# A gated recurrence in tiles of 128 tokens: a seventh pairing level and four state steps instead of eight

## The chip, the cores and the metric

The kernel runs on one core of a Trainium2 chip: TensorE (PE; its weight loads are shown apart as PEld), VectorE (DVE), ScalarE (ACT), GpSimd (POOL), and SyncE (SP), which issues most DMAs. The metric is the device time of one execution, in microseconds (us).

## The reference, cut to what matters

Two layers of an encoder with three token mixers side by side (A: latent attention, B: a gated linear recurrence, C: differential attention), gates, a projection, and a gated MLP. 512 prompt tokens and 8 requests of 16 sample tokens go through every layer, 640 tokens in all. The change is in branch B alone. Per head (8 heads, 64 key and 64 value channels), with f the forget gate of a token and channel:

```
def step(S, blk):
    qb, kb, vb, gb = blk                          # gb = log f
    b = jnp.cumsum(gb, axis=1)
    o_inter = jnp.einsum('blhk,bhkv->blhv', qb * jnp.exp(b), S)
    dec = ...                                     # exp(b_t - b_s) for s <= t, else 0
    att = jnp.einsum('bthk,btshk,bshk->bhts', qb, dec, kb)
    o_intra = jnp.einsum('bhts,bshv->bthv', att, vb)
    S = jnp.exp(b_last)[..., None] * S + jnp.einsum(
        'bshk,bshv->bhkv', kb * jnp.exp(b_last[:, None] - b), vb)
```

So a state S of 64x64 per head is carried from block to block; inside a block each token sees the earlier ones through weights that hold the decays between them. How long a block is does not change the result.

## The kernel before, in words

**The streams.** Each layer is written as four streams: A, B, C and G (the gates' projections, `stream_g`). The string `ORDER` says which stream is advanced next. What is written is not yet the order of execution: the tile framework plans each engine's queue from the dependencies, its own costs and the free buffers, earlier written work first. Each engine then runs its queue in order. So projections (line 123, groups of 24 matmuls of 320 or 256 columns, fp32 split into a high and a low part) stand between the recurrence's matmuls wherever the planner saw a gap. After the streams come the mix (branch projections under their gates, lines 1112 to 1149), the output projection and the MLP.

**Branch B** (`stream_b`) goes over two units of four heads, and in each over two pairs of heads: eight pairs over two layers. The two heads of a pair lie in the upper and lower 64 partitions of q, k and the decays F, tokens along the free dimension (640). `qz` holds q twice, each time zero in the other head's partitions.

*Levels* (lines 978 to 1002). Within blocks of 64 tokens the weights are built by doubling. At level H (1, 2, 4, 8, 16, 32) the right half of a block of 2H sees its left half: matmuls of k against qz (line 985, 64 columns each) give all weights of a chunk, a predicated copy (line 990) takes those of this level into `at`, then q of the right halves is multiplied by the decay of the left (line 995, one head on VectorE, one on GpSimd), k of the left halves by the decay of the right (line 996), and the decays of two halves are multiplied (line 998). `at` holds the weights as [128, 10, 64]: for each token tile and head the 64x64 block of either chunk.

*Chunks* (lines 1006 to 1034). q of both heads is added into one tile, k is transposed (line 1011) and copied to `kt_`. Eight chunks of 64 follow: what the state gives to the chunk (line 1021), weights times values for each head (line 1023), the state's increase (line 1026), and on VectorE for each head the new state (line 1031: old state times decay plus increase; line 1033 in the first chunk). The matmuls of a chunk use the upper or the lower 64 partitions of a tile. After that come norm, output, and the sample requests' states (lines 1035 to 1080).

Buffers come from rings by tag: `pd` has 13 of [128, 640], `sc` three banks of PSUM, `a` three tiles. `copy` (line 90) goes to ScalarE and VectorE in turn.

Of the kernel before, what the change touches and what calls it, by code (L numbers as in the profile page):

```python
# [19 lines left out]
SEQ = 512  # L20
# [10 lines left out]
class Cols:  # L31
    """tiles [128, n], one a block, read as one [128, k, n]."""
# [21 lines left out]
def body(ctx: ExitStack, tc: tile.TileContext, i, o, depth=DEPTH):  # L54
# [74 lines left out]
    def norm_T(xs, gsrc, xh, xl, stag="st"):  # L129
        """rms of token-major halves xs[h] [128, NT, 512] -> split transposed xh, xl, each [128, 4, TOK] x2; a tile a call."""  # L130
        gb = [T("e", [128, 512]) for _ in range(2)]
        for h in range(2):
            SY.dma_start(gb[h][:], gsrc[h * 512:(h + 1) * 512].partition_broadcast(128))

        def tile_(t):
            st = T(stag, [128, 16])
            cs = slice(t * 128, (t + 1) * 128)
            for h in range(2):
                A.activation(xh[h][:, :, cs], xs[h][:, t].rearrange("p (k n) -> p k n", k=4), AF.Square, accum_out=st[:, h:h + 1])
            V.tensor_tensor(st[:, 2:3], st[:, 0:1], st[:, 1:2], op=ALU.add)  # L140
            rstd(st[:, 3:4], st[:, 2:3], D)
            for h in range(2):
                xn = T("t", [128, 512])
                V.scalar_tensor_tensor(xn[:], xs[h][:, t], st[:, 3:4], gb[h][:], op0=ALU.mult, op1=ALU.mult)  # L144
                ps = P("tp")
                for k in range(4):
                    PE.transpose(ps[:, k * 128:(k + 1) * 128], xn[:, k * 128:(k + 1) * 128], ident[:])  # L147
                pv = ps[:].rearrange("p (k n) -> p k n", k=4)
                hi = xh[h][:, :, cs]
                if isinstance(xl[h], Cols):  # L150
                    A.copy(hi, pv)
                    for k in range(4):
                        V.tensor_tensor(xl[h][:, k, cs], pv[:, k], hi[:, k].bitcast(F32), op=ALU.subtract)  # L153
                else:
                    split(hi, xl[h][:, :, cs], pv)
        return tile_
# [4 lines left out]
    def projB(w, c0, xh, xl, evac, tag="mm", hs=(0, 1)):  # L161
        """feature-major: columns c0..c0+128 of the unit, all tokens in two halves."""
        for h in hs:
            ps = P(tag)
            prs = []
            cs = slice(h * HT, (h + 1) * HT)
            for u in range(len(w)):
                hi, lo = w[u]
                for k in range(4):
                    a, b = hi[:, k, c0:c0 + 128], lo[:, k, c0:c0 + 128]  # L170
                    prs += [(a, xh[u][:, k, cs]), (a, xl[u][:, k, cs]), (b, xh[u][:, k, cs])]
            mm3(ps[:, :HT], prs)
            evac(h, ps[:, :HT])
# [10 lines left out]
    def tok_out(l, t, name, ap_fn):  # L184
        """DMA a token tile: prompt rows or sample rows."""

    def constants():
# [28 lines left out]
        # hgrn lower bound: softmax over depth, running sum less the first  # L216
# [30 lines left out]
    for l in range(depth):  # L247
# [15 lines left out]
        # ---- input norm  # L263
# [21 lines left out]
        def put_T(dst_, cols, tok):  # L285
            """transpose a token-major [128, 512] tile into feature-major columns."""
            ps = P("tp")
            for k in range(4):
                PE.transpose(ps[:, k * 128:(k + 1) * 128], tok[:, k * 128:(k + 1) * 128], ident[:])
            copy(dst_[:, :, cols], ps[:].rearrange("p (k n) -> p k n", k=4))  # L290

        def headnorm(on, ps, n, st, rs=None):
            """rms over groups of 64 of ps [128, n * 64] (PSUM), each over its rs where given, without the gain."""
            sq = T("t", [128, 512])
            A.activation(sq[:, :n * 64], ps, AF.Square)
            V.tensor_reduce(st[:, 0:n], sq[:, :n * 64].rearrange("p (h d) -> p h d", d=64), axis=AX.X, op=ALU.add)
            scaled_rstd(st[:, 0:n], n, rs)
            V.tensor_tensor(on, ps.rearrange("p (h d) -> p h d", d=64), bc(st[:, 0:n], 64), op=ALU.mult)

        def scaled_rstd(v, n, rs):  # L300
            """rstd of v / rs^2 over 64, times 1 / rs (rs in its first n columns, the next n are scratch)."""
            if rs is None:
                rstd(v, v, 64)
                return
            r = rs[:, n:2 * n]
            V.reciprocal(r, rs[:, 0:n])
            for _ in range(2):
                V.tensor_tensor(v, v, r, op=ALU.mult)
            rstd(v, v, 64)
            V.tensor_tensor(v, v, r, op=ALU.mult)  # L310
# [6 lines left out]
        # == gates  # L317
        gpark = {}

        def stream_g():  # L320
            """branch gates, parked in DRAM until their branch is there."""
            for n in (0, 2, 1):
                for u in range(4):
                    wg = wload2(W_in, C_G + n * D + u * 256)
                    for c in range(2):
                        sg = T("g", [128, TOK])

                        def ev(h, ps):
                            A.activation(sg[:, h * HT:(h + 1) * HT], ps, AF.Tanh, scale=0.5)
                        projB(wg, c * 128, xh, xl, ev)  # L330
                        gp = dp.tile([128, TOK], F32, name=f"gp{l}_{n}_{2 * u + c}", tag=f"gp{l}_{n}_{2 * u + c}")[:]
                        SY.dma_start(gp, sg[:])
                        gpark[n, 2 * u + c] = gp
                    yield

        # ---- branch A: latent attention
        def stack_k(dst_, src):
            """32 rows of keys as 96: high, high, low (against queries' high, low, high)."""
# [4 lines left out]
        def stream_a():  # L343
# [48 lines left out]
            def a_latents(t):  # L392
# [13 lines left out]
                # rotary key  # L406
# [7 lines left out]
                # queries  # L414
# [19 lines left out]
            for t in range(NT):  # L434
# [5 lines left out]
                for hf in range(2):  # L440
# [21 lines left out]
                    else:  # L462
# [4 lines left out]
                        for bq in range(2):  # L467
                            # rows: high, low, high
# [26 lines left out]
            # == A keys and values  # L495
# [48 lines left out]
            # == A prompt attention  # L544
# [28 lines left out]
            # == A sample requests, against the latent rows  # L573
# [81 lines left out]
        # ---- branch C: differential attention  # L655
        def stream_c():
# [21 lines left out]
            def c_inproj(u):  # L678
                """queries and keys of two blocks; high and low parts of the prompt's go to DRAM."""
# [44 lines left out]
            def c_stack(blk, hh):  # L724
                """a head's two queries and keys as 96 rows: high, low, high against high, high, low."""
# [11 lines left out]
            # == C prompt attention  # L737
# [4 lines left out]
            def p_probs(un, q):  # L742
                """a head's weights for a block of queries, over the first softmax's scale."""
# [59 lines left out]
            # == C sample requests  # L803
# [69 lines left out]
            for bh in range(2):  # L873
# [8 lines left out]
                # each row holds two heads' values; its own half counts  # L882
# [22 lines left out]
        # ---- branch B: gated recurrence  # L905
        def stream_b():
            ob = kept["ob"] = T("ob", [128, 4, TOK])
            late = None
            for u in range(2):
# [39 lines left out]
                for c in range(2):  # L949
# [5 lines left out]
                    # == B diagonal and levels  # L955
# [18 lines left out]
                    # qz holds each head's q (zero in the other head's rows) with its decay from the start of its block, k that to the end of its block, F a block's whole decay  # L974
# [3 lines left out]
                    for li, H in enumerate(LEVELS):  # L978
# [23 lines left out]
                        fo += nb  # L1002
                    if late:
                        late()
                    yield
                    G.tensor_tensor(q[:], qz[c][:, 0], qz[c][:, 1], op=ALU.add)
                    # == B chunks
# [10 lines left out]
                    for ch in range(SEQ // 64):  # L1018
                        t, cs = ch // 2, slice(ch % 2 * 64, ch % 2 * 64 + 64)
                        if ch:  # L1020
                            PE.matmul(ov[cs, t * 128:(t + 1) * 128], lhsT=q[:, ch * 64:(ch + 1) * 64], rhs=S[:], start=True, stop=False)
                        for hh in range(2):
                            PE.matmul(ov[cs, t * 128 + hh * 64:t * 128 + (hh + 1) * 64], lhsT=at[cs, 2 * t + hh],
                                      rhs=hv_[t][cs, c * 128 + hh * 64:c * 128 + (hh + 1) * 64], start=(ch == 0), stop=(ch == 0 or hh == 1))
                        sp = P("tp")
                        PE.matmul(sp[:, :128], lhsT=kt_[cs, t], rhs=hv_[t][cs, c * 128:(c + 1) * 128], start=True, stop=True)
                        Sn = Sbd[2 * c + ch % 2]
                        for hh in range(2):
                            hs = slice(hh * 64, (hh + 1) * 64)
                            if ch:  # L1030
                                V.scalar_tensor_tensor(Sn[hs, hs], S[hs, hs], Fc[hs, ch:ch + 1], sp[hs, hs], op0=ALU.mult, op1=ALU.add)
# [21 lines left out]
                    # == B sample states  # L1053
# [30 lines left out]
        # the branches and gates are traced interleaved, each string's letter advancing its own  # L1084
# [27 lines left out]
        # == mix: branch projections under their gates  # L1112
# [38 lines left out]
        # ---- output projection and residual  # L1151
# [22 lines left out]
        # ---- gated MLP with causal convolution  # L1174
# [89 lines left out]
        # == down projection  # L1264
# [9 lines left out]
        for s in range(2):  # L1274
# [13 lines left out]
            # the token tiles end one after the other  # L1288
# [18 lines left out]
    # ---- final norm  # L1307
# [75 lines left out]
```

## Time and profile before

| | us |
|---|---|
| median of 3 runs | 2901.35 (2899.43 to 2904.15) |
| span of the profiled execution | 2904.4 |
| its own time around the span | not shown by the page |
| PE busy / PEld busy | 2835.3 / 2542.7 |
| DVE / ACT / POOL busy | 1472.6 / 987.4 / 352.5 |

A matmul in fp32 shows as two instructions (64 matmuls of a line appear as x128). Matmuls are pipelined and their ends are modelled, so that in an order of time the distance from start to start is the cost, not the duration. The page's slices:

```profile
PE   7999999999999999999999999999999999999998
DVE  5465464355565544443454654633646545444444
PEclk9999999999999999999999999999999999999999
```

Each digit is a fortieth of the span (73 us) in tenths. Layer 0's recurrence lies from 622 to 839 us (slices 9 to 12), layer 1's from 2060 to 2270 (slices 29 to 32). The eight pairs, as the sums below take them, are 622 to 668, 668 to 709, 765 to 805, 805 to 839, 2060 to 2100, 2100 to 2142, 2193 to 2233 and 2233 to 2270 us; between the units lie projections alone.

### The profile page before, as it was taken

The numbers are of one execution on the slowest core, as the hardware profiler recorded it, in microseconds if no ns is written. First come the engines' busy times: TensorE is split into PE (matmuls) and PEld (weight loads), VectorE is DVE, ScalarE is ACT, GpSimd is POOL, SyncE is SP. The second block draws the span as 40 slices with busy tenths as digits, with TensorE's granted clock in tenths as the row PEclk, the third lists the DMA queues.
The fourth block names the chain that finished last, engine by engine and source line by source line (L and its number), as shares of the span: only waits on it lengthen the run. The fifth ranks groups of instructions, "written<-read, shape, count | busy, mean of one in ns | idle before, by whom it ended". The sixth has DMA issues, their size and how long they took to land. (4 is left out here: it accounts for less than half of the span.)

```text
span 2904.4 us, 48551 instructions
## 1 busy us (share of the span) xinstructions
PE 2835.3 (98%) x19600; PEld 2542.7 (88%) x19600; DVE 1472.6 (51%) x3117; ACT 987.4 (34%) x2074; POOL 352.5 (12%) x559
## 2 busy tenths in 40 slices
PE   7999999999999999999999999999999999999998
PEld 7979997778889999998899799977788899999976
DVE  5465464355565544443454654633646545444444
ACT  4444453232221322222444443623222223222332
POOL 1000120012122001000000011200222210110000
PEclk9999999999999999999999999999999999999999
DMA  4213563322244222222333136443232442222222
GB/s 147 69 50 110 169 173 115 118 89 82 80 140 155 74 73 73 73 85 76 98 110 93 41 120 184 122 141 116 82 98 66 154 134 70 73 77 81 86 73 73
DMA packets 297996, 293.66 MB, mean 101 GB/s; under 512 B 51493, under 2 KB 254765, under 8 KB 296237
## 3 DMA queue, kind: packets, MB, share of 16 engines
q1 hardware_dynamic: 290092, 277.97, 31.1%
q0 software_dynamic: 7680, 12.59, 1.8%
q8 instruction: 155, 2.54, 0.4%
q14 instruction: 69, 0.56, 0.1%
HBM read 245.37 MB, written 44.09 MB: 100 GB/s over the span
## 5 line engine op out<-in xcount | busy, mean ns | idle before, releaser
L99 DVE TENSOR_TENSOR wl<-wr,wh 128x1024 fp32r<-128x1024 f32 (+2 forms) x292 | 370.6, 1270 | 339.1 <-ACT wh L98 336.3
L98 ACT CAST wh<-wr 128x1024 fp32r<-128x1024 f32 (+2 forms) x292 | 305.1, 1045 | 605.9 <-PE sc L123 213.0
L123 PE MATMUL mm<-xh,wh 128*128 128x320 f32 x1280 | 409.0, 320 | 0.0
L123 PE MATMUL mm<-xl,wh 128*128 128x320 f32 x1280 | 408.1, 319 | 0.0
L123 PE MATMUL mm<-xh,wl 128*128 128x320 f32 x1280 | 405.2, 317 | 0.0
L123 PE MATMUL sc<-ob,wh 128*128 128x320 f32 x1568 | 400.6, 310 | 2.9 <-DVE pd L1142 2.9
L123 PE MATMUL mm<-wh,xh 128*128 128x256 f32 (+1 forms) x960 | 281.2, 293 | 6.6 <-ACT xh L1148 3.9
L123 PE MATMUL mm<-wh,xl 128*128 128x256 f32 (+1 forms) x960 | 280.4, 292 | 1.1 <-DVE xl L99 1.0
L123 PE MATMUL mm<-wl,xh 128*128 128x256 f32 (+1 forms) x960 | 280.8, 293 | 0.0
L123 PEld LDWEIGHTS sc<-ob,wh 128*128 128x128 f32 x1568 | 275.1, 188 | 3.7 <-DVE pd L1142 3.7
L123 PE MATMUL mm<-ob,wh 128*128 128x320 f32 (+1 forms) x1088 | 275.1, 312 | 1.2 <-ACT ob L98 0.6
L123 PE MATMUL sc<-ob,wl 128*128 128x320 f32 x832 | 257.6, 310 | 0.0
L123 PEld LDWEIGHTS mm<-xh,wh 128*128 128x128 f32 x1280 | 243.0, 190 | 7.2 <-issue 3.1
L123 PEld LDWEIGHTS mm<-xh,wl 128*128 128x128 f32 x1280 | 242.6, 190 | 6.3 <-issue 3.4
L123 PEld LDWEIGHTS mm<-xl,wh 128*128 128x128 f32 x1280 | 242.9, 190 | 4.9 <-issue 0.4
L123 PE MATMUL mm<-ob,wl 128*128 128x320 f32 (+1 forms) x720 | 224.7, 312 | 0.0
L123 PE MATMUL sc<-pd,wh 128*128 128x320 f32 x608 | 189.3, 311 | 3.4 <-DVE pd L1142 3.4
L123 PEld LDWEIGHTS mm<-wh,xh 128*128 128x128 f32 x960 | 184.1, 192 | 9.3 <-ACT xh L1148 4.3
L123 PEld LDWEIGHTS mm<-ob,wh 128*128 128x128 f32 x1088 | 189.4, 188 | 2.9 <-DVE ob L99 1.1
L123 PEld LDWEIGHTS mm<-wh,xl 128*128 128x128 f32 x960 | 183.8, 192 | 1.7 <-DVE xl L99 1.2
L123 PEld LDWEIGHTS mm<-wl,xh 128*128 128x128 f32 x960 | 184.1, 192 | 1.1 <-issue 0.8
L123 PEld LDWEIGHTS sc<-ob,wl 128*128 128x128 f32 x832 | 156.2, 188 | 0.0
(379 smaller groups left out, 5218.3 us busy)
## 6 DMA issues: line engine op xcount, KB each, us to landing
wr<-in_w_in_dram SPq DMA_DIRECT2D x104, 512.0 KB, 4.2
wr<-in_ffn_w_up_dram SPq DMA_DIRECT2D x88, 512.0 KB, 3.6
wr<-in_ffn_w_down_dram SPq DMA_DIRECT2D x44, 512.0 KB, 3.6
pd<-in_cache_diff_k_dram SPq DMA_DIRECT2D x64, 256.0 KB, 3.8
pd<-in_cache_diff_v_dram SPq DMA_DIRECT2D x64, 256.0 KB, 3.2
gp<-g SPq DMA_DIRECT2D x48, 320.0 KB, 3.8
pd<-gp SPq DMA_DIRECT2D x48, 320.0 KB, 3.8
wr<-in_w_branch_dram SPq DMA_DIRECT2D x24, 512.0 KB, 3.6
```

The source lines that it names most:

```text
L98: a = A.copy(hi, src)
L99: v = V.tensor_tensor(lo, src, hi.bitcast(F32), op=ALU.subtract)
L123: PE.matmul(out, lhsT=a, rhs=b, start=(j == 0), stop=(j == n - 1))
```

## The change

After the sixth level a seventh joins the two chunks of a tile. Four matmuls (one a tile, both heads' q of the right chunk against k of the left) go into one bank of PSUM. The weights then get a buffer of their own for each head, `ap_[z]` [128, 4, 128], from the ring `pd`: ScalarE copies the two diagonal blocks of 64x64 from `at` (for all tiles at once), GpSimd sets the lower left block to zero, and `copy` takes the upper right one from PSUM. q of the right chunks, k of the left ones and the decays are updated as at any level. The chunk loop then has four steps over tiles of 128 tokens: reading the state, weights times values and the state's increase each use all 128 partitions. What is written for the sample requests, which end at level 8, is the same. The rest of the diff takes comments and docstrings out.

```diff
@@ -1000,11 +1000,32 @@
                             tot = fx[:, fo + SEQ // 16:fo + SEQ // 16 + NB]
                         Fc = Fn
                         fo += nb
+
+                    ps = P("sc")
+                    for t in range(4):
+                        PE.matmul(ps[:64, t * 128:(t + 1) * 128], lhsT=k[:, t * 128:t * 128 + 64], rhs=qz[c][:, :, t * 128 + 64:(t + 1) * 128],
+                                  start=True, stop=True)
+                    ap_ = [T("pd", [128, 4, 128]) for _ in range(2)]
+                    for z in range(2):
+                        az = at[:, 0:8].rearrange("p (t z) n -> p z t n", z=2)[:, z]
+                        for ch in range(2):
+                            r = slice(ch * 64, (ch + 1) * 64)
+                            A.copy(ap_[z][r, :, r], az[r])
+                        G.memset(ap_[z][64:128, :, 0:64], 0.0)
+                        copy(ap_[z][0:64, :, 64:128], ps[:64].rearrange("p (t z n) -> p z t n", t=4, z=2)[:, z])
+                    fv = Fc[:, :8].rearrange("p (n two) -> p n two", two=2)
+                    v4 = lambda tl: tl[:, :SEQ].rearrange("p (n two h) -> p n two h", two=2, h=64)
+                    for z in range(2):
+                        qv = v4(qz[c][:, z])[:, :, 1]
+                        (G if z else V).tensor_tensor(qv, qv, bc(fv[:, :, 0], 64), op=ALU.mult)
+                    V.tensor_tensor(v4(k)[:, :, 0], v4(k)[:, :, 0], bc(fv[:, :, 1], 64), op=ALU.mult)
+                    Fc = fx[:, fo:fo + 4]
+                    V.tensor_tensor(Fc, fv[:, :, 0], fv[:, :, 1], op=ALU.mult)
                     if late:
                         late()
                     yield
                     G.tensor_tensor(q[:], qz[c][:, 0], qz[c][:, 1], op=ALU.add)
-                    # == B chunks
+
                     kt_ = T("e", [128, NT, 128])
                     tp = P("tp")
                     for t in range(4):
...
@@ -1015,20 +1036,19 @@
                     copy(kt_[:, 4], tp[:, :128])
                     ov = P("ov")
                     S = None
-                    for ch in range(SEQ // 64):
-                        t, cs = ch // 2, slice(ch % 2 * 64, ch % 2 * 64 + 64)
-                        if ch:
-                            PE.matmul(ov[cs, t * 128:(t + 1) * 128], lhsT=q[:, ch * 64:(ch + 1) * 64], rhs=S[:], start=True, stop=False)
+                    for t in range(4):
+                        if t:
+                            PE.matmul(ov[:, t * 128:(t + 1) * 128], lhsT=q[:, t * 128:(t + 1) * 128], rhs=S[:], start=True, stop=False)
                         for hh in range(2):
-                            PE.matmul(ov[cs, t * 128 + hh * 64:t * 128 + (hh + 1) * 64], lhsT=at[cs, 2 * t + hh],
-                                      rhs=hv_[t][cs, c * 128 + hh * 64:c * 128 + (hh + 1) * 64], start=(ch == 0), stop=(ch == 0 or hh == 1))
+                            PE.matmul(ov[:, t * 128 + hh * 64:t * 128 + (hh + 1) * 64], lhsT=ap_[hh][:, t],
+                                      rhs=hv_[t][:, c * 128 + hh * 64:c * 128 + (hh + 1) * 64], start=(t == 0), stop=(t == 0 or hh == 1))
                         sp = P("tp")
-                        PE.matmul(sp[:, :128], lhsT=kt_[cs, t], rhs=hv_[t][cs, c * 128:(c + 1) * 128], start=True, stop=True)
-                        Sn = Sbd[2 * c + ch % 2]
+                        PE.matmul(sp[:, :128], lhsT=kt_[:, t], rhs=hv_[t][:, c * 128:(c + 1) * 128], start=True, stop=True)
+                        Sn = Sbd[2 * c + t % 2]
                         for hh in range(2):
                             hs = slice(hh * 64, (hh + 1) * 64)
-                            if ch:
-                                V.scalar_tensor_tensor(Sn[hs, hs], S[hs, hs], Fc[hs, ch:ch + 1], sp[hs, hs], op0=ALU.mult, op1=ALU.add)
+                            if t:
+                                V.scalar_tensor_tensor(Sn[hs, hs], S[hs, hs], Fc[hs, t:t + 1], sp[hs, hs], op0=ALU.mult, op1=ALU.add)
                             else:
                                 V.tensor_copy(Sn[hs, hs], sp[hs, hs])
                         S = Sn
```

## Rows read from the trace of the kernel before

**Rows 1.** the page's busy times: busy us, share of the span, instructions.
```profile
PE 2835.3 (98%) x19600; PEld 2542.7 (88%) x19600; DVE 1472.6 (51%) x3117; ACT 987.4 (34%) x2074; POOL 352.5 (12%) x559
```

**Rows 2.** table by stage, sums over the eight pairs; all engines, then line 123.
```profile
sum 320.00, PE 306.16 PEld 249.97 DVE 213.39 ACT 68.13 POOL 94.75; mean PE 38.27 PEld 31.25 DVE 26.67 ACT 8.52 POOL 11.84
...
sum 320.00, PE 162.12 PEld 133.09; mean PE 20.27 PEld 16.64
```

**Rows 3.** order of time on PE, end of layer 0's recurrence (start, us, instruction).
```profile
838.94 0.27 PE L1049 MATMUL tp<-ident,t 128*128 128x128 f32 x1
838.96 0.54 PE L123 MATMUL sc<-ob,wh 128*128 128x320 f32 x2
```

**Rows 4.** order of time on PE, one chunk step of the first pair.
```profile
650.73 0.43 PE L1021 MATMUL ov<-Sbd,pd 128*64 128x128 f32 x2
651.09 0.44 PE L1023 MATMUL ov<-ob,a 64*64 64x64 f32 x4
651.47 0.48 PE L1026 MATMUL tp<-ob,e 64*128 64x128 f32 x2
651.88 0.41 PE L123 MATMUL mm<-xl,wh 128*128 128x320 f32 x1
```

**Rows 5.** order of time on PE, runs of full-array fp32 matmuls.
```profile
228.77 1.14 PE L634 MATMUL tp<-a,pd 128*128 128x128 f32 x8
229.74 0.39 PE L634 MATMUL tp<-a,ckv 128*128 128x128 f32 x2
229.97 1.06 PE L634 MATMUL tp<-a,pd 128*128 128x128 f32 x8
230.86 0.39 PE L634 MATMUL tp<-a,ckv 128*128 128x128 f32 x2
```

**Rows 6.** costliest groups on PE: out<-in, shapes, count | busy us, mean ns | idle before.
```profile
L568 PE MATMUL ov<-a,pd 128*64 128x128 f32 x320 | 31.4, 285 | 0.0
L1023 PE MATMUL ov<-ob,a 64*64 64x64 f32 x256 | 29.2, 236 | 0.0
L1026 PE MATMUL tp<-ob,e 64*128 64x128 f32 x128 | 26.2, 331 | 0.0
L1021 PE MATMUL ov<-Sbd,pd 128*64 128x128 f32 x112 | 25.0, 307 | 0.1
```

**Rows 7.** costliest groups on DVE, ACT and POOL, same columns.
```profile
L1031 DVE SCALAR_TENSOR_TENSOR Sbd<-Sbd,e,tp 64x64 f32<-64x64 f32 x112 | 31.3, 279 | 45.4 <-PE tp L1026 42.9
L995 DVE TENSOR_TENSOR qz<-qz,e 128x256 f32<-128x256 f32 x16 | 10.2, 640 | 0.0
L996 DVE TENSOR_TENSOR pd<-pd,e 128x256 f32<-128x256 f32 x16 | 6.6, 412 | 0.0
L95 DVE COPY t<-sc 64x256 f32<-64x256 f32 x4 | 1.6, 406 | 0.0
L998 DVE TENSOR_TENSOR e<-e 128x8 f32<-128x8 f32 x8 | 1.3, 160 | 0.1
...
L93 ACT COPY t<-sc 64x256 f32<-64x256 f32 x4 | 1.4, 360 | 0.8 <-PE sc L1059 0.8
...
L995 POOL TENSOR_TENSOR qz<-qz,e 128x256 f32<-128x256 f32 x16 | 10.4, 651 | 25.5 <-PE sc L985 17.3 <-issue 5.0 <-DVE e L998 1.7
L840 POOL MEMSET e<- 128x128 f32 x32 | 6.6, 206 | 303.4 <-PE tp L860 172.6 <-DVE e L850 88.5 <-ACT a L93 12.5
```

**Rows 8.** order of time on PE: a level that waits, and a step at half clock.
```profile
670.68 0.82 PE L985 MATMUL sc<-qz,pd 128*64 128x64 f32 x20 [0.56 <-DVE pd L996]
...
690.48 0.69 PE L1021 MATMUL ov<-Sbd,pd 128*64 128x128 f32 x2
...
692.43 0.69 PE L1021 MATMUL ov<-Sbd,pd 128*64 128x128 f32 x2
```

**Rows 9.** table by stage: slice, length, PE, PEld, DVE, ACT, POOL, clock, DMA share, GB/s.
```profile
690.00:700.00 10.00, 10.00 (x49) 6.88 (x47) 1.96 (x7) 1.64 (x2) 0.00 (x0) 0.50 0.02 3
...
2140.00:2150.00 10.00, 10.00 (x74) 10.00 (x74) 1.58 (x6) 2.26 (x6) 0.70 (x1) 0.83 0.55 199
```

More of the change, by code (lines that the diff above doesn't have):

```diff
@@ L184, in tok_out @@
     def tok_out(l, t, name, ap_fn):
+        pass
     def constants():
```

## The prediction

> **What bounds the kernel now.** Three views, in this order. First the page's busy times [rows 1]: TensorE is busy for 98% of the span, VectorE for half, ScalarE for a third, GpSimd for an eighth. So the first question about any edit is what it does to TensorE's own work. Second, the table by stage over the eight stretches in which a pair of heads goes through the recurrence, four in each layer [rows 2]: 320 us, TensorE busy 306 of them, so it stands for 14 us only; VectorE 213, ScalarE 68, GpSimd 95. The same table for the projection line alone shows why: 162 of the 306 us are matmuls of the projections that the planner laid between the recurrence's own. They go on to the end: 20 ns after the stretch's last transpose the branch projections begin [rows 3]. There is always something to put into a gap, so the time of this stage is the sum of TensorE's work, and a microsecond of it saved is a microsecond of the whole. Third, the order of time on TensorE within a chunk step [rows 4]: reading the state, weights times values and the new state's product follow each other without a gap, 1.15 us for the eight instructions of a step (each fp32 matmul shows as two).
>
> **What the state steps cost and will cost.** Now: eight steps a pair at 1.15 us, less the state product that the first step lacks (0.37): 8.8 us of TensorE. Each of the three groups uses part of the array (128x64, 64x64, 64x128) and every change from one to the next shows: two instructions of 128 columns take 0.36 to 0.41 us.
> After: four tiles of 128 tokens, all on the full array, 6 + 3 x 8 = 30 instructions. The full-array row with as many columns is the latent attention's output [rows 5]: eight instructions from 228.77 to 229.74 (0.121 each), eight from 229.97 to 230.86 (0.111). So 30 instructions cost 3.3 us at the least. At the most each tile costs what a step's groups cost today, with the weights' four at 0.45: 4 x 1.23 - 0.37 = 4.6. I take 3.9 (0.13 each): the rows of full-array runs are nearer, since all three groups now have one shape, but the groups stay short and are entered from 320-column projections.
>
> The Trainium skill, TensorEngine Tiling (Array Packing), section Key Properties, says that a change of tiling mode drains the engine. By that rule alone a tile would cost eight times 0.111, 0.9 us, and the gain would grow by some 4 us over the eight pairs; the trace agrees in kind (0.18 to 0.2 us an instruction where the mode changes, 0.11 where it does not) [rows 4, 5].
>
> **The new level.** Four matmuls a pair, eight instructions, 64 columns of weights against 128 columns. No row shows this shape alone. From below: prompt attention's 128*64 form, two halves side by side, 31.4 us busy for 320, 0.10 each [rows 6], 0.8 us. From above: 0.18 each as in the state product [rows 4] and 0.2 for getting in and out, 1.7 us. I take 1.3.
> TensorE per pair: 8.8 - 3.9 - 1.3 = 3.6 us saved; ends 8.8 - 3.3 - 0.8 = 4.7 and 8.8 - 4.6 - 1.7 = 2.5. Times eight pairs: 29 us, ends 20 to 38.
>
> **Work on the other engines, per pair** [rows 7]. VectorE loses eight state updates of 0.28 (2.2 us) and gains one multiply on q (0.64), one on k (0.41), the decay product (0.16) and one of the two copies out of PSUM (0.41): 1.6. ScalarE gains four copies of 64x256 and the other copy out of PSUM, at 0.36 each 1.8 us; it is idle four fifths of this stage. GpSimd gains its multiply (0.65) and two fills, each between the 128x128 fill's 0.21 and that multiply's 0.65: at most 2 us on an engine that is idle two thirds. None becomes the bound, so I cost them at nothing. What hides them is projections; where that cover is gone (a layer's last microseconds) they cost at most their own chain once a layer, under 3 us in all.
>
> **Waits that are added.** In TensorE's queue the new matmuls wait for the sixth level's q and k, then the weights-times-values matmuls wait for ScalarE's copies, and the transposes of k wait for the extra multiply on k. Behind each stand projections, and for those wait the casts and evacuations. Today's like: at 670.68 a level's matmuls wait 0.56 us for k [rows 8]; over all, 14 us for eight pairs of six levels and a state stage, 0.25 each [rows 2]. One more level a pair: between nothing and 0.56, plus the same for the copies; I take 0.25 for each pair, 2 us. On the other side, four steps instead of eight halve the ping-pong with VectorE, but TensorE hardly stands there today, so I book nothing for it.
> No DMA is added or moved. Two more 128x512 buffers a pair come from the ring of 13 wide ones. Two pairs share a unit: it holds q, k and decays for both and two value masks each, ten; with two new ones each, fourteen, less the first pair's decays, which end with its first level. So a buffer may come free a moment late for the second pair's masks: between nothing and the 0.65 us of GpSimd's multiply, the nearest row [rows 7], which projections cover; I take nothing.
>
> **The clock.** In the second pair the steps run at half clock: 1.95 us each from 690.48 on [rows 8], while the engine had been full of short, partly filled matmuls before. The table by stage has a lowered clock in four slices of 10 us of the stage, the first and the last in [rows 9], granted 0.50, 0.82, 0.66 and 0.83: 10 + 3.6 + 6.8 + 3.4 = 24 us at 1.2 instead of 2.4 GHz. A step grows from 1.15 to 1.95 there, so 41% of the 24, 10 us, is lost. The change halves the state steps and fills the array in them, but adds one more sparse level. Ends: all 10 us back, or another 10 lost. I take 2 us back.
>
> **Sum.** 29 - 2 + 2 = 29 us less. The profiled execution has a span of 2904.4 us; the page shows no time around it, and the span lies 3 us (0.1%) above the median of the runs, 2901.35. Taken from the median: 2872.
>
> **Rivals.**
> *The joins stall TensorE (slower).* Place: between the sixth level and the first state product of each pair. TensorE's queue is in order; if the planner prices the five ScalarE copies too low, the first weights-times-values matmul stands at the queue's head for up to 1.8 us, then the transposes' copy queues behind them on ScalarE (0.6), with the level's own wait (0.56), the multiply on k (0.4) and a second head's copy through VectorE (0.4, with what is queued ahead of it up to 1.2): 4.6 us a pair, 37 in all, against 29 saved: 2909. It decides from 3.6 us a pair on. For it: ScalarE was never in this chain before. Against it: waits of this kind cost 0.25 each today, and half of TensorE's work is there to fill. 11%.
> *The saving is eaten (no change).* The same joins at 3 to 4 us, or the planner's new order costs in the next stage, which starts the moment this one ends [rows 3], what the steps save: 2896 to 2907. 9%.
> *Part-array matmuls were already cheap (slower).* If the half-size matmuls of before run beside each other, full-array ones cost twice as much: tiles at 2.3 us, 4 x 2.3 - 0.7 + 1.3 = 9.8 against 8.8, 8 us more: 2909. The trace speaks against it: four 64x64 instructions take 0.37 us, 0.09 each, and the full-array ones 0.11 [rows 4, 5]. 4%.
> The Trainium skill, TensorEngine Tiling (Array Packing), section Theoretical Speedup, is the rule behind this one: small matmuls in tiles of the array can run up to two or four times as fast.
> *The clock stays up (much faster).* All half-clock stretches of the stage vanish: 8 us more than I took, 2864. 12%.
>
> **How the numbers follow.** The forecast, with its own range of 2860 to 2888 from the ends of the terms, holds 64%. Faster by over 0.2% (5.8 us, about what a measurement of this kernel can tell from no change): 64 + 12 and a little of the no-change case, 0.77. Within 0.2%: 0.08. Slower: 11 + 4, 0.15. The range leaves out the two slower cases and the extreme of the faster one: 2855 to 2901.
>
> **What would show it.** In the changed kernel's list of groups the three lines of the state steps, 29.2 + 26.2 + 25.0 = 80 us busy now [rows 6], should come to 32 to 40 in 48 + 128 + 64 full-array instructions, and a new group of 64 to 6 to 14. A tile should take 0.9 to 1.2 us on TensorE. TensorE's idle time over the eight stretches should stay within 3 us of 14; if it grows by 25 or more, at waits for ScalarE's copies, the first rival holds. If tiles take 2 us at full clock, the third does. The granted clock in the stage shows the fourth. Outside the recurrence the stages should keep their lengths within 5 us together; if the gain or loss sits there, my reason is wrong even where the time is right.

## The result, and the profile after

The changed kernel takes 2873.92 us, the median of four runs (2870.24 to 2880.15); the kernel before, run four times beside it, 2901.89 (2899.43 to 2904.15). The ratio is 0.9897 [0.9876, 0.9919], 28 us less; the prediction was 2872.

The profiled executions give the same: a span of 2878.3 us against 2904.4, 26.1 less, and both ran at a mean granted clock of 0.988, so that the clock is no part of that difference. First the page's busy times of the changed kernel, to be read beside [rows 1].

```profile
PE 2799.7 (97%) x19408; PEld 2528.4 (88%) x19408; DVE 1469.0 (51%) x3085; ACT 1001.8 (35%) x2114; POOL 357.0 (12%) x583
```

TensorE lost 35.6 us of work and the span 26.1: some of the work that went came back as standing. ScalarE gained 14 us and GpSimd 5, which is nothing to engines that are idle for most of the span.

The costliest groups of the changed kernel (out<-in, shapes, count | busy us, mean ns of one | idle before) answer to [rows 6]. In the new numbering, reading the state is L1041, weights times values L1043, the state's product L1046, the new level L1006; L1013 are ScalarE's copies of the diagonal, and L969 and L1079 (diagonal sums and sample reads, which the change left alone) come up in the last experiment.

```profile
L1043 PE MATMUL ov<-ob,pd 128*128 128x64 f32 x128 | 18.9, 260 | 0.1
L1046 PE MATMUL tp<-ob,e 128*128 128x128 f32 x64 | 10.5, 287 | 0.0
L1041 PE MATMUL ov<-Sbd,pd 128*128 128x128 f32 x48 | 10.5, 300 | 0.8 <-DVE Sbd L1053 0.8
L1006 PE MATMUL sc<-qz,pd 128*64 128x128 f32 x64 | 8.5, 275 | 0.2
L969 PE MATMUL tp<-half,e 128*128 128x2 f32 x80 | 11.3, 266 | 0.0
L1079 PE MATMUL sc<-qz,e 128*64 128x32 f32 x128 | 8.9, 224 | 0.0
L1013 ACT COPY pd<-a 64x256 f32<-64x256 f32 x32 | 12.9, 403 | 22.7 <-DVE a L990 22.4
```

The three lines of the steps come to 39.9 us busy where they had 80.4, the level to 8.5. ScalarE idles 22.7 us before its copies, nearly all of it for the last level's weights on VectorE: the copies wait, and what matters is whether TensorE then waits for them. Its order of time in the first pair (start, us, instruction; a row may stand for several instructions) shows what two tiles take, beside [rows 4]:

```profile
651.51 0.31 PE L123 MATMUL mm<-xh,wl 128*128 128x320 f32 x1
651.81 0.46 PE L1041 MATMUL ov<-Sbd,pd 128*128 128x128 f32 x2
652.11 0.56 PE L1043 MATMUL ov<-ob,pd 128*128 128x64 f32 x4
652.50 0.44 PE L1041 MATMUL ov<-Sbd,pd 128*128 128x128 f32 x2
652.78 0.56 PE L1043 MATMUL ov<-ob,pd 128*128 128x64 f32 x4
653.17 0.66 PE L1046 MATMUL tp<-ob,e 128*128 128x128 f32 x4
653.59 0.39 PE L123 MATMUL mm<-xh,wh 128*128 128x320 f32 x1
```

From start to start, reading the state takes 0.30 and 0.28 us, weights times values 0.39, the products of two tiles 0.42: 0.9 us for a tile of 128 tokens, where a chunk of 64 took 1.15.

Next the table by stage, from some 5 us before each layer's first recurrence matmul to the end of the mix, longer than the eight pairs of [rows 2] because the planner now carries work over their ends (stretch, length, then busy time of PE, PEld, DVE, ACT, POOL, granted clock, DMA share, GB/s). Before:

```profile
622.50:927.60 305.10, 296.10 (x2339) 266.01 (x2336) 180.53 (x348) 70.20 (x113) 78.24 (x62) 0.97 0.37 117
2057.40:2360.60 303.20, 292.07 (x2361) 264.11 (x2357) 183.72 (x347) 70.07 (x113) 78.10 (x63) 0.99 0.37 117
```

After:

```profile
623.20:912.90 289.70, 276.77 (x2242) 258.79 (x2240) 179.27 (x331) 77.42 (x133) 83.27 (x75) 0.98 0.40 123
2045.00:2336.00 291.00, 278.57 (x2266) 260.38 (x2263) 182.53 (x332) 77.44 (x133) 81.20 (x75) 0.98 0.40 122
```

The two stretches shrank from 608.3 to 580.7 us, by 27.6; all the rest of the span went from 2296.1 to 2297.6. So the gain sits in the recurrence and nowhere else. In the stretches TensorE's busy time fell from 588.2 to 555.3, and its standing rose from 20.1 to 25.4. Counted from start to start over every instruction of the two stretches, less the idle time, the steps went from 68.4 to 25.1 us, and the level added 7.9. What TensorE stood for in layer 0 (engine line waited for: us, times, longest):

```profile
PE sc L123 <- DVE pd L1162: 2.7, 2, 2.3
PE sc L985 <- DVE pd L996: 2.4, 2, 1.4
PE tp L1085 <- DVE t L95: 2.2, 2, 2.1
PE ov L1207 <- DMA g<-in_state_ffn_conv_dram: 1.5, 1, 1.5
...
PE ov L1041 <- DVE Sbd L1053: 0.4, 1, 0.4
```

The same view of before:

```profile
PE sc L123 <- DVE pd L1142: 3.0, 3, 1.4
PE sc L985 <- DVE pd L996: 2.1, 3, 1.4
PE tp L1065 <- DVE t L95: 1.4, 2, 1.0
```

None of it is for the new copies. The added 5.2 us in both layers are 2.3 at the transposes for the MLP's convolution (L1207), 1.7 at the levels' matmuls, 0.7 at the state reads, 0.6 at the sample transposes; the small rest falls and rises elsewhere. Before, two of those four transposes a layer stood in these stretches too (at 852.8 and 2284.0 us) and waited for nothing; now they come at 828.4 and 2251.2, close behind their own DMA. The first transfer of their input is issued 3.7 and 2.8 us ahead of them, where before it was issued 10.0 and 9.4 us ahead.

### The profile page after: what moved, and what is told of

The parts are those of the page before. It is cut to its first block, busy times and chain, and to the rows that moved or that the text cites. A ratio compares the mean times of both kernels' runs of the same rounds, so it can differ in the third digit from the quotient of the medians.

```text
span 2878.3 us, 48206 instructions
## 1 busy us (share of the span) xinstructions
PE 2799.7 (97%) x19408; PEld 2528.4 (88%) x19408; DVE 1469.0 (51%) x3085; ACT 1001.8 (35%) x2114; POOL 357.0 (12%) x583
```

## The experiments

The theory: TensorE's instructions in the steps are the bound, and the change halves their number and ends the changes of array shape between them. Rivals: the time sat in the chain of states between TensorE and VectorE; the shapes alone set it, not the number; the joins cost what the steps save.

Runs that are compared shared a chip with runs of before. The mean granted clock of single executions varies, so where a few us matter I compare at one clock: over 48 executions of before the time falls by 2.35 us for each 0.001 of mean granted clock, over 14 of the changed kernel by 2.32. At 0.990 before takes 2903.4 us and the changed kernel 2876.4, 27.0 less. "At equal clock" below means this. It leaves out whatever an edit does through the clock itself.

**The changed kernel again,** as the base of the first runs below.

> The changed kernel once more, as the base for the three beside it. Theory (the gain is TensorE's own work in the state steps, about 36 us less in the steps and the new level together, with some 7 us of new standing time and a clock that gives nothing back): 2870 to 2880, ratio to the kernel before 0.988 to 0.992. Rival (the gain of the first runs was the clock's luck): a ratio above 0.995 or below 0.985, moving with the granted clock.

2876.33 us against 2907.6, ratio 0.9881 [0.9854, 0.9909]: the gain repeats on another chip.

**Twice the instructions at the full array.** Each matmul of a tile step is cut along its moving columns, so that the steps have 60 instructions a pair, two fewer than before (the 62 of the expectation is before's number).

> The changed kernel, but every matmul of the four tile steps is cut in two along its moving columns: 62 instructions a pair instead of 30, as many as before the change, all on the full array; the sums are the same. Theory 1 (a short fp32 instruction costs about 0.105 to 0.12 us on TensorE however few columns it moves, so the number counts): 32 more instructions a pair, 3.4 to 3.8 us, 27 to 31 us in all: 2900 to 2905, the whole gain gone. Theory 2 (what was dear before was the part-array shapes and the changes between them): 0.055 us an instruction of half the columns, so 0 to 8 us: 2873 to 2882.

```diff
+ for ch in range(2):
+     co = t * 128 + ch * 64
+     if t:
+         PE.matmul(ov[:, co:co + 64], lhsT=q[:, t * 128:(t + 1) * 128], rhs=S[:, ch * 64:(ch + 1) * 64], ...)
+     for j in range(2):
+         PE.matmul(ov[:, co + j * 32:co + (j + 1) * 32], lhsT=ap_[ch][:, t], ...)
+     PE.matmul(sp[:, ch * 64:(ch + 1) * 64], lhsT=kt_[:, t], ...)
```

2901.79 us, ratio 0.9977 [0.9963, 0.9990]: nine tenths of the gain are gone, +24 us at equal clock. Its groups (columns as above):

```profile
L1046 PE MATMUL ov<-ob,pd 128*128 128x32 f32 x256 | 38.5, 275 | 0.1
L1044 PE MATMUL ov<-Sbd,pd 128*128 128x64 f32 x96 | 19.2, 283 | 0.0
L1048 PE MATMUL tp<-ob,e 128*128 128x64 f32 x128 | 18.8, 280 | 0.0
```

Half the columns cost as much as all: 275 to 283 ns against 260 to 300 in the changed kernel. From start to start 480 instructions took 54.1 us, 0.107 each where the clock was full (26 of them ran at the lower level), against 0.105 for the 240. So at the full array the number of instructions sets the time, and the moving columns, from 32 to 128, do not. That the shapes alone set it falls too: 480 at 0.107 are 51.5 us, and before's 496 take 64.1 at full clock (below), so by this estimate the one shape gives about a third of what the steps save and the smaller number two thirds.

**The same number in halves of the array.** Now each matmul is cut along its weight columns, 64 and 64, the two halves in turn.

> The changed kernel, but every matmul of the four tile steps is cut in two along its weight columns, 128x64 on the left and right half of the array in turn: 62 instructions a pair, one tiling mode throughout; the sums are the same. If halves run side by side as in prompt attention (0.067 us an instruction of 128 columns) and as in the levels (0.037 with 64 columns): 30 x 0.067 + 32 x 0.04 = 3.3 us a pair against 3.15 now, 0 to 5 us more: 2872 to 2880. If the number of instructions alone counts (0.105 to 0.12 each): 27 to 31 us more, 2900 to 2905.

```diff
+ h2 = [slice(ch * 64, ch * 64 + 64) for ch in range(2)]
...
+     for cs in h2:
+         PE.matmul(ov[cs, t * 128:(t + 1) * 128], lhsT=q[:, t * 128 + cs.start:t * 128 + cs.stop], rhs=S[:], ...)
+ for hh in range(2):
+     for cs in h2:
+         PE.matmul(ov[cs, ...], lhsT=ap_[hh][:, t, cs], ...)
+ for cs in h2:
+     PE.matmul(sp[cs, :128], lhsT=kt_[:, t, cs], ...)
```

2881.55 us, ratio 0.9904 [0.9881, 0.9927], +4.9 at equal clock.

```profile
L1047 PE MATMUL ov<-ob,pd 128*64 128x64 f32 x256 | 17.5, 227 | 0.1
L1044 PE MATMUL ov<-Sbd,pd 128*64 128x128 f32 x96 | 10.2, 290 | 0.0
L1050 PE MATMUL tp<-ob,e 128*64 128x128 f32 x128 | 10.1, 279 | 0.0
```

The same 480 instructions cost 27.5 us here, 0.057 each, so "number" alone is too coarse a reason. In order of time (columns as above):

```profile
651.18 0.40 PE L1047 MATMUL ov<-ob,pd 128*64 128x64 f32 x8
651.41 0.39 PE L1044 MATMUL ov<-Sbd,pd 128*64 128x128 f32 x4
651.63 0.40 PE L1047 MATMUL ov<-ob,pd 128*64 128x64 f32 x8
```

Eight instructions of 64 moving columns take 0.23 us, four of 128 take 0.22. Within these rows an instruction for one half starts 6 or 7 ns behind its neighbour for the other, and the next two follow 0.058 us after them with 64 moving columns and 0.11 with 128. So the two halves run side by side, and with 64 weight columns the moving columns do count.

The Trainium skill, TensorE: Matmul & The Clock Gate, section LDWEIGHTS, says that a weight load costs by its columns alone, columns/1.2 in ns: 107 for 128 columns, 53 for 64. The 0.105 to 0.107 us of the full array and the 0.058 of two halves with 64 moving columns agree with it; the 0.11 with 128 moving columns is more than such a load.

Before paid 0.129 for each of its 496 at full clock, in three shapes that take turns. Of the +4.9 the projections between the steps took 3 (435.5 us of line 123 in the changed kernel's stretches, 438.4 here). I put that down to entering them from another shape, which was not tried by itself.

**Weights times values twice.** The matmuls are issued twice, the second overwriting the first.

> The changed kernel with the weights-times-values matmuls of each tile issued twice (the first result is overwritten): 128 more full-array instructions on TensorE, no other engine's work changed, no new wait. Theory (in this stage a microsecond on TensorE is a microsecond of the whole, since projections fill every gap): 128 x 0.094 to 0.11 = 12 to 14 us more: 2885 to 2890. Rival (the stage's length is set by the chain through VectorE and the state, and TensorE's work lies beside it): 0 to 4 us more.

```diff
+ for hh in range(2):
+     PE.matmul(ov[:, t * 128 + hh * 64:...], lhsT=ap_[hh][:, t], rhs=hv_[t][...], start=True, stop=True)
```

2889.62 us, ratio 0.9935 [0.9914, 0.9957], +15.3 at equal clock.

```profile
L1041 PE MATMUL ov<-ob,pd 128*128 128x64 f32 x128 | 19.9, 267 | 0.1
L1046 PE MATMUL ov<-ob,pd 128*128 128x64 f32 x128 | 18.1, 264 | 0.0
```

From start to start the steps rose by 13.6 us, 0.106 for each of 128 added instructions, and all of it reached the end: nothing hides TensorE's work in this stage.

**Before, with half of the state updates.** VectorE's update is left out in every second chunk, so that later chunks read a state that lacks it.

> The kernel before, all eight state steps on TensorE, but VectorE updates the state only in every second chunk: the update of the odd chunks is left out (so later chunks read a state that lacks it). That is the change's saving on VectorE (64 updates of 0.28 us fewer, and half of the ping-pong with TensorE) without its saving on TensorE. Theory (TensorE's work sets the stage): 0 to 3 us faster, 2898 to 2902. Rival (the shorter chain of state updates made the gain): 15 to 25 us faster, 2876 to 2887.

```diff
+ if ch % 2:
+     continue
- Sn = Sbd[2 * c + ch % 2]
+ Sn = Sbd[2 * c + ch // 2 % 2]
```

2901.6 us against 2907.24, ratio 0.9984 [0.9969, 0.9999]; at equal clock +0.3. Halving the chain of states alone gives none of the 15 to 25 us that the rival wanted: it falls. The 5.6 us in the medians go with a higher granted clock (0.991 against 0.988 on this chip); whether the edit raised it, the run does not tell. This run serves for another thing too. Its steps had the full clock throughout:

```profile
L1023 PE MATMUL ov<-ob,a 64*64 64x64 f32 x256 | 28.2, 230 | 0.0
L1021 PE MATMUL ov<-Sbd,pd 128*64 128x128 f32 x112 | 24.2, 298 | 0.0
L1026 PE MATMUL tp<-ob,e 64*128 64x128 f32 x128 | 23.4, 322 | 0.0
```

From start to start 64.1 us against 68.4 in before's profile, of which some ran at half clock [rows 8].

**Before, with the level's matmuls, copies and fills on top.** They stand after the sixth level, with the four copies on ScalarE, the two fills and the two copies out of PSUM of the change. Their result is not used; the level's multiplies are not added.

> The kernel before with the seventh level's four matmuls, the four copies by ScalarE, the two fills by GpSimd and the two copies out of PSUM added after the sixth level, their result not used, all eight steps as before (the multiplies on q and k are left out). The price of the addition by itself. Theory: 64 instructions at 0.125 us, 8 us, and 0 to 4 us of standing: 2909 to 2914. Rival (the joins with ScalarE stall TensorE): 20 us or more, above 2921. If it is hidden: below 2904.

```diff
+ ps = P("sc")
+ for t in range(4):
+     PE.matmul(ps[:64, t * 128:(t + 1) * 128], lhsT=k[:, t * 128:t * 128 + 64], rhs=qz[c][...], ...)
+ ap_ = [T("pd", [128, 4, 128]) for _ in range(2)]
...
```

2922.73 us, ratio 1.0059 [1.0035, 1.0083], +14.9 at equal clock, between what the theory (8 to 12) and the rival (20 and more) wanted.

```profile
L1005 PE MATMUL sc<-qz,pd 128*64 128x128 f32 x64 | 8.7, 279 | 0.0
```

Its matmuls cost 8.2 us from start to start, standing in the stage rose by 2.7, the projections by 2.8. So nearly half of the level's price was not its own work; whether this much came with it in the changed kernel, where the steps behind it differ, the run does not tell.

**The copies twice.** Each of ScalarE's four diagonal copies is issued twice.

> The changed kernel with each of ScalarE's four diagonal copies issued twice: 1.4 us more on ScalarE in each of eight pairs, between the sixth level and the first weights-times-values matmul. Theory (the join is covered by projections): 0 to 2 us more than the changed kernel. Rival (TensorE stands for ScalarE's copies): 8 to 11 us more.

```diff
- A.copy(ap_[z][r, :, r], az[r])
+ for _ in range(2):
+     A.copy(ap_[z][r, :, r], az[r])
```

2868.96 us, ratio 0.9874 [0.9853, 0.9894]; at equal clock −0.7.

```profile
L1014 ACT COPY pd<-a 64x256 f32<-64x256 f32 x64 | 25.8, 403 | 13.0 <-DVE a L990 11.8
```

12.9 us more of copies between the level and the steps change nothing: TensorE has other work until they are done. The join is not a cost.

**The level in both halves, samples on the full array.** The level's matmuls go to the upper and lower PSUM half in turn; the sample tile's weights move into the full buffer (two matmuls of 128x128 instead of four of 64x64).

> A version meant to beat the changed kernel. The seventh level's matmuls of two tiles go to the lower and the upper half of PSUM's partitions in turn, so that they can run side by side on the array's two column halves (0.067 us an instruction instead of 0.125: 8 x 0.058 x 8 = 3.7 us less), with four smaller copies out of PSUM instead of two; and the sample tile's weights get the same full buffer, so that two full-array matmuls a pair take the place of four of 64x64 (32 instructions fewer, 2 to 3 us). Theory: 4 to 7 us under the changed kernel, 2867 to 2870; if the extra copies are not covered, no gain.

```diff
- PE.matmul(ps[:64, t * 128:(t + 1) * 128], lhsT=k[...], ...)
+ PE.matmul(ps[t % 2 * 64:(t % 2 + 1) * 64, t // 2 * 128:(t // 2 + 1) * 128], lhsT=k[...], ...)
...
- for ch in range(2): PE.matmul(ov[cs, ...], lhsT=at[cs, 8 + hh], ...)
+ PE.matmul(ov[:, hh * 64:(hh + 1) * 64], lhsT=ap_[hh][:, 4], ...)
```

2869.99 us, ratio 0.9876 [0.9853, 0.9900]; at equal clock −0.9, nothing. The halves in turn took the level from 7.9 to 4.7 us, but the sample matmuls rose from 4.5 to 5.4, and the sample states' product after them from 9.8 to 12.3. That product also varies, from 7.5 to 11.7, between versions that leave it and the sample matmuls as they are, so the runs show only in part what took the gain back. The first part of the edit was kept, the second was not.

**The changed kernel once more,** beside the last one.

> The changed kernel again, on the chip of the next one, as its base: 2868 to 2878; by the runs so far 2.4 us less for each 0.001 that the mean granted clock is higher, 2876 at 0.990 and 2871 at 0.992.

2877.94 us, ratio 0.9909 [0.9889, 0.9929].

**Halves in turn wherever 64 weight columns are used.** The level, the diagonal sums (each cut into two of 64 weight columns) and the sample reads.

> A version meant to beat the changed kernel by what the 128x64 pieces showed (0.056 us an instruction where the two column halves are used in turn, 0.105 to 0.125 where one half or the full array is): the seventh level's matmuls go to the two halves in turn (8.0 us now, 4.6 in the trace of the version before this one: 3.4 less), the diagonal's matmuls are cut in two along their weight columns (8.8 us now in 80 instructions; 160 at 0.037 to 0.056, 5.9 to 9.0: up to 2.9 less), and the sample states' reads go to the two halves in turn (7.2 us in 128 instructions; at 0.037, 4.7: 2.5 less). Sum 3 to 9 us under the changed kernel at the same granted clock. If the extra copies out of PSUM or the planner's new order cost what this saves, as in the version before this one: no gain.

```diff
- PE.matmul(dps[:, 2 * t:2 * t + 2], lhsT=qk[:, t * 128:(t + 1) * 128], rhs=half2[:], ...)
+ for e in range(2):
+     PE.matmul(dps[e * 64:(e + 1) * 64, 2 * t:2 * t + 2], lhsT=qk[:, t * 128 + e * 64:t * 128 + (e + 1) * 64], ...)
...
- PE.matmul(ip[:64, b * 2 * NS:(b + 1) * 2 * NS], lhsT=S0[:, b], ...)
+ PE.matmul(ip[b % 2 * 64:(b % 2 + 1) * 64, b // 2 * 2 * NS:(b // 2 + 1) * 2 * NS], lhsT=S0[:, b], ...)
```

2863.34 us, ratio 0.9857 [0.9835, 0.9879]: 14.6 under the changed kernel beside it in the medians, 8.1 at equal clock. It is the fastest version here.

```profile
L970 PE MATMUL tp<-half,e 128*64 128x2 f32 x160 | 6.0, 200 | 0.0
L1082 PE MATMUL sc<-qz,e 128*64 128x32 f32 x128 | 5.3, 225 | 0.0
L1007 PE MATMUL sc<-qz,pd 128*64 128x128 f32 x64 | 5.3, 282 | 0.2
```

The sample reads (L1079 in the changed kernel, L1082 here) are the clean pair: as many instructions of the same shape, 0.22 us each by their own duration in both, but from start to start 7.3 us into one half and 3.9 into the two in turn, 0.057 against 0.030. Here too the halves run side by side. The three lines together fell by 11.1 us; standing rose by 5.6, which took back part of it.

## Why the prediction was right

**What bounds the stage.** That its time is the sum of TensorE's work held: 13.6 us more of it cost 15.3, while 12.9 us more of copies cost nothing and a halved chain of states gained nothing at equal clock. The rest of the span moved by 1.5 us, within the 5 that were allowed.

**The steps.** 70 us before was 68.4 (64.1 where the clock stayed up); 31 after was 25.1. Here the size was off: I took 0.13 us for an instruction, above the rows of full-array runs [rows 5], since short groups entered from projections might cost more. They don't: 0.105. The lower end, 0.111, was the better value. (The first step of before lacks the reading of the state, 0.36, and not the product, 0.37 [rows 4]; the sum does not feel it.)

The Trainium skill's TensorEngine Tiling (Array Packing), section Key Properties, says that a change of mode drains the engine. The tile of 0.9 us that the prediction gave for steps without such changes is what the trace shows. That the rows of before agreed in kind was read from two of the three groups: the four 64x64 instructions took 0.38 us, 0.09 each [rows 4].

The three lines came to 39.9 us busy in 48 + 128 + 64 instructions, as foretold (32 to 40), and the tile of 0.9 us lies at the low end of the 0.9 to 1.2 that I gave it.

**The level.** 10.4 us predicted, 7.9 measured, inside its bounds. Steps and level together gave 68.4 − 25.1 − 7.9 = 35.4 us where I had 29; against steps at full clock, 64.1, it is 31.

**The waits.** I took 2 us and allowed 3 more of standing; it rose by 5.2 (over the longer stretch). The mechanism that I named, the levels' q and k, makes 1.7 of it; for ScalarE's copies TensorE never stands. The largest part, 2.3, is the convolution's transposes, which now follow their DMA too closely. "No DMA is added or moved" was true of the source and not of the plan. The run of before with the level on top stands 2.3 us at the same transposes; the one with half of the updates has them behind the stage, at 982 us in layer 0, and does not wait. So the level's work in the plan is enough to bring this wait. Why the planner moves them was not tried.

**The other engines.** ScalarE's copies took 0.40 us each instead of 0.36, and cost nothing, as booked; no wait of TensorE's leads to the fills or to a buffer of the ring.

**The clock.** I took 2 us back. In the profiled pair it gave nothing: over the two stretches of the table by stage both kernels have about 27 us at the lower level of 1.2 GHz (in before the four slices of the prediction, 24 us [rows 9], are most of them), though in the changed kernel no instruction of the steps fell into them. Two of its slices (same columns as the table by stage):

```profile
790.00:800.00 10.00, 10.00 (x72) 9.34 (x68) 6.02 (x14) 0.86 (x3) 3.89 (x4) 0.63 0.18 54
2210.00:2220.00 10.00, 10.00 (x62) 9.12 (x62) 6.47 (x15) 1.04 (x3) 3.75 (x3) 0.52 0.16 53
```

Over all executions its mean granted clock was 0.9903 against 0.9884, worth 4.5 us by the slope above; so the sign held, and the size is within what single executions scatter. What in the change moves the clock was not tried.

**The sum.** −29 + 2 − 2 was predicted; the profiles give −35.4 (steps and level), +5.2 (standing), +2.6 (other lines of the stage and rounding), +1.5 (elsewhere): −26.1. The 2 us between forecast and median are closer than the terms were, and that is in part luck: 6.4 us too little in the saved work was made up by 3.2 too little in the waits, 4.1 in lines and stages that had no term, and the 2 of the clock that the profiled pair lacks.

**The rivals.** The joins: not there (the doubled copies). The saving eaten: a seventh of it was, by standing, not all. Part-array matmuls already cheap: its mechanism exists, as halves in turn show, but before's steps had little of it, with 0.129 an instruction in changing shapes. The Trainium skill, TensorEngine Tiling (Array Packing), section Theoretical Speedup, names up to two or four times, and those steps were nowhere near. The clock staying up: not in the profiled pair.

## What to carry to other kernels

Where an in-order engine is full and other work fills its gaps, price an edit by that engine's instructions alone, and let chains and copies on idle engines be free until a run shows otherwise. Price short fp32 matmuls by the instruction: at the full array its moving columns, up to 128, cost nothing, with 64 weight columns they do. Keep runs of them in one array shape; with 64 weight columns, send neighbours to the two halves in turn. And look where the planner puts the later work after an edit: a wait that was none may become one.

## What was not expected of the hardware

A full-array fp32 instruction costs 0.105 to 0.107 us with 32, 64 or 128 moving columns, and the 128x2 ones of the diagonal sums no less (9.9 us for 80 in before, 0.124). With 64 weight columns and neighbours in one half it was 0.057 (32 moving columns, the sample reads) to 0.124 (128, the level); with halves in turn 0.030 (32) to 0.073 (128). Inside a group of these runs the distance goes by the larger of the two numbers of columns: 0.112 with 128 weight columns whatever the moving ones, 0.109 with 64 and 128, 0.058 with 64 and 32; halves in turn give two instructions in that time.

The same kernel on one core does not always get the same clock: the mean granted clock of an execution of before ran from 0.983 to 0.993, and 0.010 of it is 24 us, nearly as much as the whole change. Two medians of a few runs can therefore differ by some us without any cause in the code, as the 14.6 and 8.1 us of the last experiment do.
